# GpSimd's passes over normed rows and over q and k in pieces of 256 columns, and the q/k norm's factor inside the power

## The chip, the core and the metric

The kernel runs on one core of a Trainium2 chip. The time is the device time of one execution in microseconds; the median of several runs is compared. An execution of its own is taken with the hardware profiler and gives the trace.

## What is computed

One layer of a bidirectional encoder trunk for two groups of requests, a prompt of 4096 rows and a sample of 2048 rows, each of 1024 columns. Cut to what matters:

```python
def layer_norm(x, g, b):
    mu = x.mean(-1, keepdims=True)
    var = jnp.square(x - mu).mean(-1, keepdims=True)
    return (x - mu) * lax.rsqrt(var + 1e-5) * g + b

def l2norm(t):                       # each head's 64 values of q and of k
    return t * lax.rsqrt(jnp.sum(t * t, -1, keepdims=True) + 1e-6)

def mixer_layer(x, mem, w_in, ...):
    h = x @ w_in                     # one projection, split among three groups of heads
    y_attn = window_attention(aq, ak, av, sink, rel_bias) * silu(az)   # 8 heads, band of 3 blocks of 128
    y_dn = deltanet_branch(dn_q, dn_k, dn_v, a, b, ...) * silu(dn_z)   # short_conv, silu, l2norm(q), l2norm(k)
    y_mem = memory_attention(mq, mem @ w_mem_kv) * silu(mz)
    return concatenate([y_attn, y_dn, y_mem]) @ w_out

x = layer_norm(x, ln_in_g, ln_in_b); mem = layer_norm(mem, ln_in_g, ln_in_b)
x = layer_norm(2 ** 0.25 * x + mixer_layer(x, mem, ...), ln_g, ln_b)
```

## The kernel before

The 6144 rows are 48 tiles of 128 rows, handled in 24 pairs; another four tiles are the memory rows.

**The first part** (to about 1440 us) goes over the pairs. For each tile, `front` (from line 819) loads 1024 columns of f32 into `x` (three buffers), takes the statistics on VectorE (`bst`, `bmv`), the power of the variance on GpSimd (`brs`), the scale and shift on ScalarE, and then the gain and the bias in two passes on GpSimd over all 1024 columns (lines 825 and 826, the tiles `x<-x,grow` and `x<-x,brow`). ScalarE rounds the rows to f16 and VectorE takes the rest (`xhl`); a DMA transposes both (`xT`). `proj` (line 1235) multiplies with the weights on TensorE (`psf`, `psq`, `psk`). `attention` (line 1305) makes logits (`pslg`), adds the bias and takes the maximum on VectorE (`lg`, `mx`), the exponential on ScalarE, splits into two f16 halves (`aphl`), transposes by DMA (`apt`) and multiplies with v (`psov`). `conv` (line 1414), for the pair before, runs the five-tap convolution on VectorE (`acc`), silu, the split (`cfh`), a DMA transpose (`raw`), and for each tile the norm of q and k (lines 1434 to 1455): GpSimd adds the two halves (`n<-raw`, two passes of 256), ScalarE squares, VectorE sums 64 at a time and adds eps (`nss`), GpSimd takes the power -1/2 of 8 values per row, VectorE multiplies them by 1024, GpSimd multiplies 512 columns by them (`n<-n,nss`), and the result is split (`kqtm`) and stored. GpSimd also adds up v (`v<-raw`).

**The second part** runs both directions of the delta rule with their triangular inverses on GpSimd (`nb`, `tb`), the gates, the memory attention, the output projection (`pso`) and the last norm. None of its instructions is in the diff.

**The order.** No engine instruction is issued as it is written down. `Plan` (from line 56) collects the operations of a part with their dependences, gives each a cost from formulas (on GpSimd 200 ns plus 2.1 ns for each column, or 1.66 with a broadcast operand; a power 348 ns plus 165 for each column), and sorts them by a list scheduler, one queue for each engine and one for SyncE's DMAs; ranks come from a run backwards, seven schedules are made, and the one with the shortest planned end is issued. Its formulas have no term for engines that hold each other off. A list is ordered and issued when a pool closes: once for the first part (line 1620), once for the second. Each engine works its queue strictly in order. All instructions carry line 505, where the sorted list is issued; in the views they are told apart by their tiles.

Of the kernel before, what the change touches and what calls it, by code (L numbers as in the profile page):

```python
# [14 lines left out]
ALU = mybir.AluOpType  # L15
# [4 lines left out]
P = 128  # L20
D = 1024
# [529 lines left out]
def encoder(ctx: ExitStack, tc: tile.TileContext, A, outs):  # L551
    nc = tc.nc
    plan = Plan(tc)
    V, S, G, T, Q = plan.engines()
# [21 lines left out]
    def sc1(name):  # L576
        nscal[0] += 1
        return scal[:, nscal[0] - 1:nscal[0]]
# [212 lines left out]
    def layer_norm_stats(pool, x, eps, tag):  # L791
        st = pool.tile([P, 2, 6], F32, tag=tag + "st", name="bst")
        for i in range(2):
            V.bn_stats(st[:, i, :], x[:, i * 512:(i + 1) * 512])
        mv, rs = norm_scale(pool, st, eps, tag)
        nb = pool.tile([P, 1], F32, tag=tag + "nb", name="bnb")
        V.scalar_tensor_tensor(nb, mv[:, 0:1], -1.0, rs, op0=ALU.mult, op1=ALU.mult)
        return rs, nb
# [9 lines left out]
    def split(eng_hi, dst_h, dst_l, src, scale=None):  # L808

        if scale is None:  # L810
            S.activation(dst_h, src, AF.Copy)
            V.tensor_tensor(dst_l, src, dst_h, op=ALU.subtract)
        else:
            S.activation(dst_h, src, AF.Copy, scale=scale)
            V.scalar_tensor_tensor(dst_l, src, scale, dst_h, op0=ALU.mult, op1=ALU.subtract)

    grow_in, brow_in = grow, brow

    def front(pool, src_rows, xT_out, hl_dram=None, x_dram=None):

        x = gx.tile([P, D], F32, tag="x", name="x", bufs=3)
        Q.dma_start(out=x, in_=src_rows)
        rs, nb = layer_norm_stats(pool, x, LN_EPS, "f")
        S.activation(x, x, AF.Identity, scale=rs, bias=nb)
        G.tensor_tensor(x, x, grow_in, op=ALU.mult)
        G.tensor_tensor(x, x, brow_in, op=ALU.add)
        hl = pool.tile([P, 2, D], F16, tag="xhl", name="xhl", bufs=1)
        split(None, hl[:, 0, :], hl[:, 1, :], x)
        flat = hl.rearrange("p a b -> p (a b)")
        if xT_out is not None:  # L830
            Q.dma_start_transpose(out=xT_out, in_=flat)
        if hl_dram is not None:
            Q.dma_start(out=hl_dram, in_=flat)
        if x_dram is not None:
            Q.dma_start(out=x_dram, in_=x)
# [264 lines left out]
    def front_tile(t):  # L1100
        src = seqs[seq_of[t]][0][pos_of[t] * P:(pos_of[t] + 1) * P, :]
        front(pa, src, xT_of[t // 2][:, t % 2], x_dram=x32_d[t])
        if t % 2:
            Q.dma_start(out=xT_d[t // 2], in_=xT_of[t // 2])
# [91 lines left out]
    eps_k = sc1("eps_k")  # L1196
# [217 lines left out]
    def conv(pp):  # L1414

        c = cb[pp]
        raws = []
        for f0 in (0, 2, 4):
            acc = pa.tile([P, 2, 256], F32, tag="acc", name="acc", bufs=2)
            for f in range(2):  # L1420
                S.activation(acc[:, f], c[:, f0 + f, 0:256], AF.Copy, scale=cw[:, f0 + f, 0:1])
                for j in range(1, 5):
                    V.scalar_tensor_tensor(acc[:, f], c[:, f0 + f, j:j + 256], cw[:, f0 + f, j:j + 1], acc[:, f],
                                           op0=ALU.mult, op1=ALU.add)
            th = pa.tile([P, 2, 256], F32, tag="cth", name="cth", bufs=1)
            S.activation(th, acc, AF.Tanh, scale=hisk)
            V.scalar_tensor_tensor(acc, th, 1.0, acc, op0=ALU.add, op1=ALU.mult)
            fh = pa.tile([P, 2, 2, 256], F16, tag="cfh", name="cfh", bufs=1)
            split(None, fh[:, 0], fh[:, 1], acc)
            raw = pa.tile([P, 2, 2, 2, P], F16, tag="raw" if f0 < 4 else "rawv", name="raw", bufs=4 if f0 < 4 else 2)  # L1430
            Q.dma_start_transpose(out=raw.rearrange("p a f t c -> p (a f t) c"),
                                  in_=fh.rearrange("p a f t -> p (a f t)"))
            raws.append(raw)
        for tb in range(2):
            t = 2 * pp + tb
            n32 = pa.tile([P, 2, 4, 64], F32, tag="n32", name="n32", bufs=1)
            sq = pa.tile([P, 2, 4, 64], F32, tag="nsq", name="nsq", bufs=1)
            ss = pa.tile([P, 2, 8], F32, tag="nss", name="nss", bufs=2)
            for i in range(2):
                G.tensor_tensor(n32[:, i].rearrange("p (f h) d -> p f (h d)", f=2), raws[i][:, 0, :, tb, :],  # L1440
                                raws[i][:, 1, :, tb, :], op=ALU.add)
            S.activation(sq, n32, AF.Square)
            V.tensor_reduce(ss[:, 0], sq.rearrange("p q h d -> p (q h) d"), axis=AX.X, op=ALU.add)
            V.tensor_scalar(ss[:, 0], ss[:, 0], eps_k, None, op0=ALU.add)
            G.tensor_tensor(ss[:, 1], ss[:, 0], nhalf.to_broadcast([P, 8]), op=ALU.pow)
            V.tensor_scalar(ss[:, 1], ss[:, 1], 1024.0, None, op0=ALU.mult)
            n3 = n32.rearrange("p q h d -> p (q h) d")
            G.tensor_tensor(n3, n3, ss[:, 1].unsqueeze(2).to_broadcast([P, 8, 64]), op=ALU.mult)
            kqtm = pa.tile([P, 4, 2, 2, 64], F16, tag="kqtm", name="kqtm", bufs=1)
            o = kqtm.rearrange("p h t s d -> p t h s d")  # L1450
            split(None, o[:, :, :, 0, :], o[:, :, :, 1, :], n32)
            v32 = pa.tile([P, 4, 64], F32, tag="v32", name="v32", bufs=1)
            G.tensor_tensor(v32.rearrange("p (f h) d -> p f (h d)", f=2), raws[2][:, 0, :, tb, :],
                            raws[2][:, 1, :, tb, :], op=ALU.add)
            Q.dma_start(out=dst_d[t], in_=kqtm)
            Q.dma_start(out=dn_d[t], in_=n32)
            Q.dma_start(out=dv_d[t], in_=v32)
# [21 lines left out]
    def dn_back(pool, psp, dr, tiles, ds, emit_out):  # L1479
        for i, (t, d) in enumerate(zip(tiles, ds)):  # L1480
            dn_level(pool, psp, dr, i % NPAR, d)
            first = pos_of[t] == 0 if dr == 0 else pos_of[t] == lens[seq_of[t]] - 1
            if first:
                dn_reset(pool)
            po = dn_chain(pool, psp, dr, d)
            emit_out(t, po)

    units = [lambda m=m: front(pa, seqs[m // 2][1][(m % 2) * P:(m % 2 + 1) * P, :], None, xm_d[m])
             for m in range(4)]

# [14 lines left out]
    for i in range(NP + 1):  # L1505
        plan.rank = RK[6]
        if i + 1 < NP:
            front_pair(i + 1)
        if i < NP:
            plan.rank = RK[0]  # L1510
            proj(i)
        plan.rank = RK[2]
        if i > 0:
            conv(i - 1)
            plan.rank = RK[3]
            attention(2 * i - 1)
        if i < NP:
            plan.rank = RK[4]
            attention(2 * i)
        plan.rank = RK[5]  # L1520
        if i == min(NP, max(NG // 2, NP - FIRST)):
            gates(0, pa, (("oat", 2), ("qktm", 2), ("nsq", 1)))
            fr += dn_front([Alias(None, early)], Alias(None, {"fr": (pj, "pw", 1)}), 0, [todo[0][1]], step=1)
        for _ in range(min(len(units), -(-len(units) // max(1, NP - 3 - i)))):
            units.pop(0)()
# [308 lines left out]
```

## Time and profile before

| | |
|---|---|
| median of three runs | 3352.14 us (3349.26 to 3354.52) |
| the profiled execution | 3363.07 us, of which the span 3361.0 us |
| TensorE matmul busy | 2870.1 us, 85% |
| VectorE busy | 2920.9 us, 87% |
| ScalarE busy | 2441.2 us, 73% |
| GpSimd busy | 1711.0 us, 51% |
| chain of waits | VectorE 31%, TensorE 20%, GpSimd 15%, DMA 13%, issue 10%, ScalarE 8% |

Busy is the time in which an engine has an instruction under way; it holds time in which that instruction itself is held up. The chain of waits goes back from the last instruction, at each step to what released it or to the instruction before it on its engine. PE is TensorE, DVE VectorE, ACT ScalarE, POOL GpSimd, SPq SyncE's queue of DMAs. `out<-in` names the tiles that an instruction writes and reads.

### The profile page before, as it was taken

What the parts mean: (1) busy time and instruction counts of PE and PEld (TensorE: products, weight loads), DVE (VectorE), ACT (ScalarE), POOL (GpSimd) and SP (SyncE); (2) the same over time, 40 slices, a digit from 0 to 9 for tenths busy, and PEclk for the clock granted to TensorE, in tenths of its full rate; (3) what the DMA queues carried; (4) which work ended last, traced back from release to release, by engine and by line L of the source; (5) the groups of instructions that cost most, each with busy time, mean ns of one, the idle gap of its engine ahead of it and who ended that gap; (6) DMA issues with size and microseconds to landing.
All of it is one profiled execution on the core that took longest, in us unless ns stands there. A gap on an engine that the chain in (4) does not pass through costs nothing.

```text
span 3361.0 us, 82755 instructions
## 1 busy us (share of the span) xinstructions
PE 2870.1 (85%) x29856; PEld 1893.3 (56%) x29856; DVE 2920.9 (87%) x6850; ACT 2441.2 (73%) x6253; POOL 1711.0 (51%) x2611
## 2 busy tenths in 40 slices
PE   5788888788898887767899999999988988998988
PEld 4566666666676665444556555555554544444544
DVE  7999868799999989678889888888878988888997
ACT  4577656767777776688888878777877777777764
POOL 3644424344444334546645455455528666657662
PEclk9899998899999998878999999999998999999999
DMA  6999999999999999898678887778788777877775
GB/s 203 239 224 220 219 222 222 234 230 220 212 233 220 200 224 247 210 223 180 165 191 194 206 181 178 172 161 181 172 190 194 191 183 179 193 179 188 183 175 154
DMA packets 1336916, 671.43 MB, mean 200 GB/s; under 512 B 1127728, under 2 KB 1243312, under 8 KB 1332280
## 3 DMA queue, kind: packets, MB, share of 16 engines
q1 hardware_dynamic: 1336504, 666.14, 86.3%
q8 instruction: 234, 3.83, 0.5%
q14 instruction: 178, 1.46, 0.1%
HBM read 240.12 MB, written 181.49 MB: 125 GB/s over the span
## 4 chain that ended last, share of the span: by engine, by line
DVE 31%; PE 20%; POOL 15%; DMA 13%; issue 10%; ACT 8%; SPq 3%; POOLq 0%; ACTq 0%; DVEq 0%
POOL nb L505 5%; DVE acc L505 5%; POOL tb L505 5%; PE pso L505 5%; PE psg L505 5%; PE psf L505 3%; SPq L505 3%; DVE lg L505 3%; DVE aphl L505 3%; PE psk L505 2%; ACT lg L505 1%; PE psq L505 1%; DMA uc<-ud 1%; PE pslg L505 1%; DVE rx L505 1%
## 5 line engine op out<-in xcount | busy, mean ns | idle before, releaser
L505 PEld LDWEIGHTS <-xT 128*128 128x128 f16 x5760 | 535.5, 99 | 385.2 <-issue 52.5
L505 PE MATMUL psg<-w2a,xT 128*128 128x512 f16 (+1 forms) x2304 | 446.0, 334 | 9.6 <-DVE qtm L505 8.0
L505 PE MATMUL psf<-xT,w1f 128*128 128x256 f16 (+1 forms) x3600 | 439.9, 276 | 14.7 <-DMA xT<-xhl 6.3
L505 PEld LDWEIGHTS <-w1f 128*128 128x128 f16 x3600 | 341.7, 101 | 59.4 <-issue 10.8
L505 POOL TENSOR_TENSOR nb<-nb,tb 128x30 f32<-128x30 f32 (+6 forms) x750 | 348.6, 465 | 49.3
L505 POOL TENSOR_TENSOR tb<-nb,na 128x30 f32<-128x30 f32 (+6 forms) x750 | 342.6, 457 | 48.3
L505 ACT ACTIVATE lg<-lg,mx,scal 128x385 f32<-128x385 f32 (+1 forms) x384 | 263.8, 688 | 122.3 <-DVE mx L505 107.6
L505 PE MATMUL pslg<-kfm,qfm 128*128 128x128 f16 x2240 | 201.0, 233 | 164.1 <-DVE mx L505 149.4
L505 DVE SCALAR_TENSOR_TENSOR acc<-cb,cw,acc 128x256 f32<-128x256 f32 x576 | 329.8, 605 | 4.1 <-POOL cb L505 1.7
L505 PEld LDWEIGHTS <-qfm 128*128 128x128 f16 x2624 | 204.2, 104 | 222.3 <-issue 188.0
L505 PEld LDWEIGHTS <-yT 128*128 128x128 f16 x2304 | 200.1, 99 | 216.1 <-issue 27.7
L505 PE MATMUL pso<-w2a,yT 128*128 128x512 f16 x1152 | 311.4, 394 | 9.6 <-DMA yT<-yhl 7.1
L505 PE MATMUL pso<-w2b,yT 128*128 128x512 f16 x1152 | 298.9, 383 | 0.0
L505 PE MATMUL psg<-w2b,xT 128*128 128x512 f16 x1152 | 289.3, 382 | 3.8 <-DMA w2b<-w_d 3.8
L505 PE MATMUL psq<-w1t,xT 128*128 128x512 f16 x1152 | 287.0, 385 | 0.2 <-ACT cb L505 0.2
L505 DVE TENSOR_TENSOR aphl<-lg,aphl 128x768 f16<-128x768 f32 (+1 forms) x192 | 209.9, 1096 | 49.7 <-ACT aphl L505 49.3
L505 POOL TENSOR_TENSOR n<-raw 128x256 f32<-128x256 f16 x96 | 82.3, 867 | 262.2 <-DMA raw<-cfh 62.1
L505 DVE CUSTOM_DVE_ANT_0 lg<-pslg,bias 128x385 f32<-128x385 f32 (+1 forms) x384 | 195.3, 539 | 17.7 <-PE pslg L505 13.5
L505 POOL TENSOR_TENSOR x<-x,grow 128x1024 f32<-128x1024 f32 x52 | 128.0, 2462 | 121.8 <-ACT x L505 117.6
L505 PEld LDWEIGHTS <-th 64*64 64x64 f16 x2304 | 99.1, 111 | 131.1 <-issue 106.1
L505 PE MATMUL psk<-w1t,xT 128*128 128x272 f16 x1152 | 161.4, 287 | 13.5 <-DVE qktm L505 10.0
L505 PE MATMUL psx<-rx,th 64*64 64x64 f16 x2304 | 126.8, 197 | 41.3 <-DVE rx L505 29.8
(1026 smaller groups left out, 7607.8 us busy)
## 6 DMA issues: line engine op xcount, KB each, us to landing
x<-x SPq DMA_DIRECT2D x48, 512.0 KB, 4.3
xT<-xT SPq DMA_DIRECT2D x24, 1024.0 KB, 5.5
xT<-xT SPq DMA_DIRECT2D x48, 512.0 KB, 4.5
n<-dn SPq DMA_DIRECT2D x96, 256.0 KB, 3.3
r<-x SPq DMA_DIRECT2D x48, 512.0 KB, 4.4
out_dram<-r SPq DMA_DIRECT2D x48, 512.0 KB, 3.8
cr<-crow SPq DMA_DIRECT2D x47, 512.0 KB, 5.1
yhl<-yhl SPq DMA_DIRECT2D x48, 384.0 KB, 3.4
```

The source lines that it names most:

```text
L505: getattr(self.eng[o["e"]], o["name"])(*o["args"], **o["kw"])
```

## The change

In `front` the two passes of 1024 columns become eight of 256, gain and bias in turn for each quarter; 52 tiles go through it. In `conv` the sum with eps is multiplied by 2^-20 in the same instruction, so that the power -1/2 gives 2^10 times what it gave; the instruction that multiplied by 1024 is gone; the pass over q and k is made in two of 256 columns, q first, then k. It is done for 48 tiles.

```diff
@@ front
         S.activation(x, x, AF.Identity, scale=rs, bias=nb)
-        G.tensor_tensor(x, x, grow_in, op=ALU.mult)
-        G.tensor_tensor(x, x, brow_in, op=ALU.add)
+        for c in range(0, D, 256):
+            xc = x[:, c:c + 256]
+            G.tensor_tensor(xc, xc, grow_in[:, c:c + 256], op=ALU.mult)
+            G.tensor_tensor(xc, xc, brow_in[:, c:c + 256], op=ALU.add)
@@ conv
-            V.tensor_scalar(ss[:, 0], ss[:, 0], eps_k, None, op0=ALU.add)
+            V.tensor_scalar(ss[:, 0], ss[:, 0], eps_k, 2.0 ** -20, op0=ALU.add, op1=ALU.mult)
             G.tensor_tensor(ss[:, 1], ss[:, 0], nhalf.to_broadcast([P, 8]), op=ALU.pow)
-            V.tensor_scalar(ss[:, 1], ss[:, 1], 1024.0, None, op0=ALU.mult)
-            n3 = n32.rearrange("p q h d -> p (q h) d")
-            G.tensor_tensor(n3, n3, ss[:, 1].unsqueeze(2).to_broadcast([P, 8, 64]), op=ALU.mult)
+            for i in range(2):
+                G.tensor_tensor(n32[:, i], n32[:, i], ss[:, 1, 4 * i:4 * i + 4].unsqueeze(2).to_broadcast([P, 4, 64]),
+                                op=ALU.mult)
```

## Rows read from the trace of the kernel before

**Rows 1.** Stages: length, PE, PEld, DVE, ACT, POOL busy, clock, DMA share, GB/s.
```profile
120.00:1320.00 1200.00, 1001.21 (x10942) 784.29 (x10941) 1076.70 (x2435) 850.26 (x2041) 510.68 (x389) 0.94 1.02 221
...
1440.00:3361.00 1921.00, 1708.61 (x17562) 1002.76 (x17562) 1667.13 (x3963) 1470.15 (x3950) 1089.34 (x2068) 0.95 0.79 183
```

**Rows 2.** Chain of waits, 120 to 1320 us, shares of that stretch.
```profile
by line: issue 14.7%; DVE acc L505 13.7%; DVE lg L505 8.0%; DVE aphl L505 7.3%; PE psf L505 6.6%; ACT lg L505 3.9%; PE psq L505 3.6%; PE pslg L505 3.0%; DVE mx L505 2.8%; DVE nss L505 2.7%; SPq L505 2.7%; DVE bst L505 2.3%; DVE cfh L505 2.1
```

**Rows 3.** Waits of PE, 120 to 1320 us: total, times, longest.
```profile
PE pslg L505 <- DVE mx L505: 136.0, 82, 8.1
PE psm L505 <- DMA wm<-wm_d: 13.2, 10, 2.9
```

**Rows 4.** Timeline, DVE and POOL near 263 us: start, length, engine, instruction.
```profile
263.08 2.36 POOL L505 TENSOR_TENSOR x<-x,brow 128x1024 f32<-128x1024 f32 x1
263.51 2.74 DVE L505 TENSOR_TENSOR aphl<-lg,aphl 128x768 f16<-128x768 f32 x1 [3.25 <-ACT aphl L505]
265.39 1.40 POOL L505 TENSOR_TENSOR n<-raw 128x256 f32<-128x256 f16 x1
```

**Rows 5.** Timeline: first and last of 96 VectorE instructions beside x passes.
```profile
12.62 3.10 DVE L505 TENSOR_TENSOR sq<-stg 128x768 bf16<-128x768 f32 x1
...
1278.53 2.40 DVE L505 SCALAR_TENSOR_TENSOR acc<-cb,cw,acc 128x256 f32<-128x256 f32 x1
```

**Rows 6.** Tile x, its passes: shortest/median/longest ns, first and last start.
```profile
L505 POOL TENSOR_TENSOR x<-x,grow x52: 2342/2366/3393, 12.2 to 1273.1; 128x1024 f32<-128x1024 f32 x52
L505 POOL TENSOR_TENSOR x<-x,brow x52: 2328/2404/3211, 15.0 to 1278.3; 128x1024 f32<-128x1024 f32 x52
```

**Rows 7.** Pieces of the chain of waits with held VectorE time, first and last.
```profile
43.07 3.25 DVE sq L505 x3
...
1273.28 2.24 DVE mx L505
```

**Rows 8.** Tile yd, its passes of 256 columns (second part).
```profile
L505 POOL TENSOR_TENSOR yd<-of,yd x48: 719/729/1742, 2521.3 to 3338.3; 128x256 f32<-128x256 f32 x48
```

**Rows 9.** Timeline: first, last VectorE instruction beside n<-raw, then beside v<-raw.
```profile
193.68 0.77 DVE L505 SCALAR_TENSOR_TENSOR acc<-cb,cw,acc 128x256 f32<-128x256 f32 x1
...
1369.46 0.90 DVE L505 SCALAR_TENSOR_TENSOR acc<-cb,cw,acc 128x256 f32<-128x256 f32 x1
...
233.65 1.42 DVE L505 TENSOR_TENSOR aphl<-lg,aphl 128x768 f16<-128x768 f32 x1
...
1419.68 0.67 POOL L505 TENSOR_TENSOR v<-raw 128x256 f32<-128x256 f16 x1
1419.76 1.14 DVE L505 TENSOR_TENSOR kqtm<-n,kqtm 128x512 f16<-128x512 f32 x1
```

**Rows 10.** Tile n, GpSimd's passes: shortest/median/longest ns.
```profile
L505 POOL TENSOR_TENSOR n<-raw x96: 661/794/2247, 128.4 to 1422.9; 128x256 f32<-128x256 f16 x96
...
L505 POOL TENSOR_TENSOR kg<-n,egs x96: 607/615/1792, 1451.3 to 2384.9; 128x256 f32<-128x256 f32 x96
...
L505 POOL TENSOR_TENSOR n<-n,nss x48: 1038/1144/1914, 146.1 to 1427.8; 128x512 f32<-128x512 f32 x48
```

**Rows 11.** Groups of POOL, 120 to 1320 us: busy us, mean ns, idle before.
```profile
L505 POOL TENSOR_TENSOR n<-raw 128x256 f32<-128x256 f16 x86 | 74.9, 881 | 229.3 <-DMA raw<-cfh 55.2 <-DVE kqtm L505 54.6 <-DMA dn<-n 39.9
```

**Rows 12.** Chain of waits, pieces of x on POOL: first and last of six.
```profile
63.12 2.33 POOL x L505
...
1190.02 2.31 POOL x L505
```

**Rows 13.** Tile nss, the multiplication by 1024.
```profile
L505 DVE TENSOR_SCALAR nss<-nss x48: 153/172/2332, 145.8 to 1427.5; 128x8 f32<-128x8 f32 x48
```

**Rows 14.** Group of DVE, 0 to 1440 us: busy, mean ns, idle before.
```profile
L505 DVE SCALAR_TENSOR_TENSOR acc<-cb,cw,acc 128x256 f32<-128x256 f32 x576 | 329.8, 605 | 4.1 <-POOL cb L505 1.7 <-ACT acc L505 1.3
```

**Rows 15.** DMA issues of the page: KB each, median us to landing.
```profile
x<-x SPq DMA_DIRECT2D x48, 512.0 KB, 4.3
...
r<-x SPq DMA_DIRECT2D x48, 512.0 KB, 4.4
```

## The prediction

> **What bounds the kernel now.** I read the busy times by stage first. The two lists that the planner orders show as two parts: the change touches only the first, which ends near 1440 us, and the 1921 us behind it are ordered from a list that the diff does not alter [rows 1]. So every term lies in 0 to 1440 us, and nearly all of it in the steady stage from 120 to 1320 us. There VectorE is busy for 1076.7 of 1200 us, TensorE for 1001.2 and GpSimd for 510.7 [rows 1]. The chain of waits of that stage is led by VectorE: acc, lg, aphl, mx, nss, bst and cfh alone give 38.9% of it [rows 2]. TensorE's largest idle cause there is VectorE emptying a logits bank (136.0 us); the largest one that is a transfer is 13.2 us [rows 3]. VectorE bounds the stage; GpSimd is idle for more than half of it.
>
> Next I read what VectorE's time is made of, in the order of time. At 263.51 us the subtraction of aphl starts beside an x pass of GpSimd and lasts 2.74 us, ending 0.81 us after the pass; the next GpSimd instruction, begun at 265.39, is drawn out to 1.40 us and ends only after aphl does [rows 4]. So the two engines hold each other off for whole instructions and take turns. Of VectorE's instructions in 0 to 1440 us that last over 100 ns longer than the median of their form, 96 overlap an x pass; 93 of the 104 passes hold one, and the excess over the medians sums to 151.6 us, or 1.46 us for each pass. The first and the last stand in [rows 5]. The median pass is 2.37 or 2.40 us [rows 6]. Traced along the chain, 80.8 us of the 151.6 lie on it, in 68 pieces, the first of them inside the sq piece and the last large one at mx [rows 7]. That is 53%.
>
> **The change, part by part.** *The x passes.* 104 passes of 1024 columns become 416 of 256. The trace has a pass of just that shape, f32 with two full operands: yd, median 729 ns [rows 8]. Four take 2.92 us where one took 2.38, so GpSimd works 416 x 0.729 - 104 x 2.38 = 56 us longer, beside an idle half.
>
> The disputed number is how long a piece holds VectorE. The trace has no x piece, so I bound it by passes of nearly this length in the same stage. The 96 passes that add raw into n (median 794 ns, shortest 661) hold VectorE for 15.6 us by the same count, 42 instructions, 162 ns a pass; the 48 that fill v from raw hold it for 13.9 us, 34 instructions, 290 ns a pass; first and last of each stand in [rows 9], the durations in [rows 10]. Scaled by 729/670 (670 being their undisturbed length, as v shows at 1419.68) these are 176 and 316 ns, and I take the middle, 246 ns: some pieces will follow each other closely as v follows n, others will stand alone. Then 416 x 0.246 = 102 us against 151.6: VectorE gains 49 us. With the 53% that lies on the chain that is **-26 us**; by the two ends 73 and 131 us are held, giving -42 and -11 us.
>
> Against it stands GpSimd's own waiting. In the stage the raw passes take 881 ns in the mean [rows 11] where the undisturbed ones take 670, so 0.2 us each is waiting for VectorE. A piece then takes 0.93 us, the eight of a tile 7.4 us against 5.0. Who waits: the copy to xhl, the transpose behind it, and whatever stands behind the pieces on GpSimd (nss, brs, n). On the chain the x passes have six pieces, 14.0 us, first and last in [rows 12]; lengthened by 49% they cost **+7 us**. The transfers and TensorE come later by at most these 2.4 us a tile, which the idle half of GpSimd and the three x buffers cover; without that cover it would be 52 x 2.4 = 125 us.
>
> The Trainium skill, "Perfetto Trace Analysis", section "Optimizing Scalar/DVE Operations", speaks against pieces: it says that grouping work into larger operations can raise throughput where the engine is saturated, because each instruction has a fixed cost. The fixed cost shows here too, by the 729 ns above; but the engine whose passes are cut is not the saturated one. If GpSimd bounded the stage the rule would decide, and the 56 us would be the sum.
>
> *The q/k norm.* The pass over q and k, 48 of 512 columns at a median of 1.14 us, becomes 96 of 256 with a broadcast operand, which kg does in 615 ns [rows 10]: +0.09 us each, 4 us of GpSimd in all, off the chain. It holds VectorE for 19.7 us now; 96 x 0.246 x 615/729 = 20 us later. Zero.
>
> *The factor.* The addition of eps takes the factor 2^-20 as its second operation, and the power gives 2^10, exact powers of two; the separate multiplication by 1024 goes. It is 48 instructions of 172 ns in the median [rows 13], 8.3 us of VectorE, also on the way from power to pass, so there is one turn from engine to engine less. Half on the chain: **-4 us**. Its longest is 2332 ns, because it too is held at times; that part is already in the sum above and moves to the instruction behind it, so it is not counted twice.
>
> *The order.* 52 x 6 + 48 - 48 instructions more, and other planned costs, mean that all of the first list is sorted anew: GpSimd, SyncE and VectorE queues may all stand in another order between 0 and 1440 us. The planner knows nothing of the holding. No row prices this; VectorE's 123 us of idle time in the stage [rows 1] is what the present order leaves, and I allow a sixth of it, 20 us, either way and zero in the sum.
>
> Sum: -26 + 7 - 4 = -23 us. On the profiled execution (span 3361.0, 3363.07 us with what lies around it) that is 3340 us; the median of the three runs is 10.9 us lower, 3352.14, and gives **3329 us**.
>
> **Rivals.** *The turn-taking eats it (slower).* When VectorE has one two-input instruction after another, as in the acc runs, every piece finds one waiting, and eight pieces hold longer than two passes do. The point from which this decides is plain: 151.6/416 = 364 ns a piece, half its length. At 450 ns the held time is 187 us, +35 us, on the chain +19; with +7 and -4 the time is 3374 us; with every piece held in full, 303 us, the same sum gives +83 us, 3435 us. For: 93 of 104 passes hold something, and after the first turn the engines are in step. Against: v, which follows other passes closely, has 316 ns scaled, and lg, bst and qktm are not drawn out, so they break the runs. The Trainium skill ("SBUF — State Buffer", section "SBUF: two separate sides") words the rule behind this rival: a VectorE instruction with two SBUF inputs and a GpSimd instruction that reads SBUF exclude one another, and whichever starts first keeps the shared ports for its whole length. The trace agrees: aphl ends behind the pass.
>
> *The gain is hidden.* The DMA engines show a mean share of 1.02 in the stage and 0.79 behind it [rows 1]. If they set the pace, or if the next stage's work on TensorE is late by as much, VectorE's 49 us only turn into idle time: 3350 us. Against: a 512 KB transfer lands in 4.3 us in the first part and in 4.4 us in the last [rows 15], so nothing queues, and TensorE hardly waits for transfers [rows 3].
>
> *More than the chain's share.* Held time off the chain delays others too. At 176 ns a piece, with all of 78 us returned and 8 us for the factor, the time is 3266 us.
>
> *The pieces don't stay together.* If the planner sorts urgent work (the power of nss, brs) between pieces, nss and brs come earlier by up to one pass; that is a gain within the forecast's range.
>
> **How the numbers follow.** The forecast case, 3293 (176 ns, order 20 us for it) to 3364 us (316 ns, order against it), has 0.57: most of it lies below 3345, so 0.51 faster and 0.06 no change. The larger gain has 0.07, the hidden gain 0.14, turn-taking 0.22 (0.21 slower, 0.01 no change). Within 0.2%, 6.7 us, is about what a measurement of this kernel can tell from no change. Faster 0.58, same 0.21, slower 0.21. The range reaches from 3280, a part of the larger gain, to 3374, the turn-taking at 450 ns; what is left out is its worse half and the best of the larger gain.
>
> **What would show it.** Right: VectorE instructions held by x pieces sum to about 100 us, none longer than 0.75 us plus its own work; acc's mean in the first part falls from 605 ns [rows 14] by some 40; the second list starts some 20 us sooner; x pieces average near 0.9 us. Wrong: held time near or over 150 us (turn-taking); held time down but the first part as long, with TensorE or ScalarE waiting for GpSimd's n, brs or x (its queue is late), or for transfers (hidden); or the first part changed by idle time of VectorE, not by its work (the order).

## The result, and the profile after

The changed kernel takes 3298.93 us in the median (3296.42 to 3300.31) beside 3350.7 us for the kernel before: a ratio of 0.9845, with a 95% interval of 0.9828 to 0.9862, or 52 us less. The forecast was 3329 us, 23 us less. Its sign was right and the time lies in its range, but the gain is 2.3 times as large as the one that was worked out. All differences in us from a run's ratio below are taken on about 3350 us; the changed kernel, measured a second time (e15), came to 58 us less by its ratio, so two such figures can differ by 6 us without a cause.

**Where the time went.** The two parts of the kernel can be timed by a landmark: the first `n64h` of the second list on ScalarE. These rows are the groups of tile n, before and then after; the columns are shortest/median/longest ns, first and last start in us.

```profile
L505 ACT ACTIVATE n64h<-n x192: 292/306/310, 1438.3 to 3299.0; 32x128 f16<-32x128 f32 x192
```
```profile
L505 ACT ACTIVATE n64h<-n x192: 292/306/310, 1383.7 to 3234.9; 32x128 f16<-32x128 f32 x192
```

The landmark comes 54.6 us sooner. The profiled execution of before was 12 us above its own median, and 9 of those us lie behind the landmark (3361.0 - 1438.3 = 1922.7 us there, 1913.9 after). On every engine the order of the second list is the same in both kernels. So the 52 us came out of the first part, as the prediction had placed it.

The same stretch by engines, up to the landmark, before and then after: length, busy us (instructions) of PE, PEld, DVE, ACT, POOL, then granted clock, DMA share, GB/s.

```profile
0.00:1438.30 1438.30, 1161.24 (x12292) 890.38 (x12292) 1252.04 (x2882) 969.36 (x2298) 621.70 (x543) 0.93 0.98 222
```
```profile
0.00:1383.70 1383.70, 1154.51 (x12292) 884.46 (x12292) 1185.96 (x2833) 971.21 (x2299) 734.28 (x903) 0.94 1.02 231
```

This is the pair of rows to read first. VectorE is busy for 66.1 us less, idle for 11.5 us more (186.3, then 197.7), and 66.1 - 11.5 is the 54.6. Some 12 of the 66.1 belong to the norm (e6 below), the others to the pieces. TensorE is busy for 7 us less and ScalarE for 2 us more, with the same work. GpSimd is busy for 113 us more, but the waits of ScalarE and VectorE for it add up to 85 us before and 89 after.

Most of what VectorE no longer loses is holding. In tile x of after, GpSimd's pieces stand where the passes of [rows 6] stood:

```profile
L505 POOL TENSOR_TENSOR x<-x,grow x208: 713/733/1717, 13.0 to 1222.2; 128x256 f32<-128x256 f32 x104
L505 POOL TENSOR_TENSOR x<-x,brow x208: 714/902/1718, 15.4 to 1223.6; 128x256 f32<-128x256 f32 x104
```

VectorE's convolution step, tile acc of after, and one of its small instructions, tile mx of before and of after:

```profile
L505 DVE SCALAR_TENSOR_TENSOR acc<-cb,cw,acc x576: 425/476/1043, 64.5 to 1333.4; 128x256 f32<-128x256 f32 x192
```
```profile
L505 DVE TENSOR_SCALAR mx<-mx,scal x96: 196/220/2318, 120.2 to 1422.6; 128x4 f32<-128x4 f32 x96
```
```profile
L505 DVE TENSOR_SCALAR mx<-mx,scal x96: 206/222/751, 110.8 to 1368.7; 128x4 f32<-128x4 f32 x96
```

The gain pieces take 733 ns in the median, nearly the 729 ns of yd [rows 8]; the bias pieces, of the same shape, take 902 ns: they too are held. acc's longest is 1043 ns, its own 476 and most of one piece; mx's longest was 2318 ns and is 751, its own 222 and less than one piece. By the count of the prediction 210 VectorE instructions are held on 193 of the 416 pieces, for 86.4 us in all, where it was 151.6. The first and the last, in the timeline of after:

```profile
13.41 1.48 DVE L505 TENSOR_TENSOR sq<-stg 128x768 bf16<-128x768 f32 x1
...
1221.61 0.69 DVE L505 TENSOR_SCALAR mx<-mx,scal 128x4 f32<-128x4 f32 x1
```

The relief is not spread evenly. By the same count aphl is held for 9.1 us instead of 26.6, mx for 9.3 instead of 19.7, cfh for 5.4 instead of 12.1. The convolution step acc hardly gains: 98 of its instructions are held for 42.7 us, half of all that is left, where 25 were held for 48.7 us. Within a run of them the two engines do take turns, as the group of acc after and one such run show (timeline of after; seven steps in 5.21 us, 744 ns each instead of 476):

```profile
L505 DVE SCALAR_TENSOR_TENSOR acc<-cb,cw,acc 128x256 f32<-128x256 f32 x576 | 319.0, 584 | 5.6 <-POOL cb L505 2.1 <-ACT acc L505 1.9
```
```profile
793.55 5.21 DVE L505 SCALAR_TENSOR_TENSOR acc<-cb,cw,acc 128x256 f32<-128x256 f32 x7
794.58 1.78 POOL L505 TENSOR_TENSOR x<-x,grow 128x256 f32<-128x256 f32 x2
796.32 1.77 POOL L505 TENSOR_TENSOR x<-x,brow 128x256 f32<-128x256 f32 x2
```

The chain of waits of the profile after breaks off 170 us before the end of the span, so it is not read here; from here on the account is VectorE's busy and idle time up to the landmark.

### The profile page after: what moved, and what is told of

Read it like the earlier page. It is cut to its first block, busy times and chain, and to the rows that moved or that the text cites. A ratio compares the mean times of both kernels' runs of the same rounds, so it can differ in the third digit from the quotient of the medians.

```text
span 3297.6 us, 83056 instructions
## 1 busy us (share of the span) xinstructions
PE 2852.4 (86%) x29856; PEld 1882.0 (57%) x29856; DVE 2852.1 (86%) x6802; ACT 2442.7 (74%) x6253; POOL 1826.1 (55%) x2971
## 5 line engine op out<-in xcount | busy, mean ns | idle before, releaser
L505 POOL TENSOR_TENSOR nb<-nb,tb 128x30 f32<-128x30 f32 (+6 forms) x750 | 356.2, 475 | 49.3
L505 DVE SCALAR_TENSOR_TENSOR acc<-cb,cw,acc 128x256 f32<-128x256 f32 x576 | 319.0, 584 | 5.6 <-POOL cb L505 2.1
L505 POOL TENSOR_TENSOR x<-x,grow 128x256 f32<-128x256 f32 x208 | 176.7, 865 | 117.4 <-ACT x L505 105.0
L505 DVE TENSOR_TENSOR aphl<-lg,aphl 128x768 f16<-128x768 f32 (+1 forms) x192 | 195.4, 1018 | 53.1 <-ACT aphl L505 52.6
L505 POOL TENSOR_TENSOR x<-x,brow 128x256 f32<-128x256 f32 x208 | 189.4, 927 | 0.0
```

Of the source, the lines that this page charges most:

```text
L505: getattr(self.eng[o["e"]], o["name"])(*o["args"], **o["kw"])
```

## Experiments

Two theories stood first. **A:** the shorter holding is the gain, in whatever order. **B:** the planner's new order is the gain. They are told apart by a square: each order with whole passes and with pieces. Where a kernel keeps an order, the planner is given the same list, and only what is issued at a place differs.

### Pieces at the old order (e1)

```diff
         G.tensor_tensor(x, x, grow_in, op=ALU.mult)      # planned as before
+        plan.ops[-1]["emit"] = pieces(grow_in, ALU.mult)  # issued as four passes of 256
...                                                        # the bias likewise
```

> The planner's list and its order are those of the kernel before; each x pass is issued at its place as four passes of 256 columns (four gains where the gain stood, four biases where the bias stood); the norm is as before. Theory A (holding): the gain comes from VectorE being held for shorter pieces, in any order. The held time beside x passes falls from 152 to 80 to 110 us and the kernel takes 3300 to 3320 us. Theory B (order): the new order of the first list made the gain. The time stays within 10 us of 3351, held time or not.

Measured: 0.9898 (0.988 to 0.9915), 34 us less. Held 91.8 us. The stretch to its landmark:

```profile
0.00:1400.80 1400.80, 1150.92 (x12292) 882.68 (x12292) 1199.58 (x2882) 971.46 (x2298) 709.83 (x855) 0.94 1.00 228
```

VectorE is busy for 52.5 us less than before, idle for 15 us more, and the part is 37.5 us shorter. Shorter holding at an unchanged order, with what GpSimd's longer work takes back, gives two thirds of the gain.

### The new order with whole passes (e2)

```diff
         for c in range(0, D, 256):
             G.tensor_tensor(xc, xc, grow_in[:, c:c + 256], op=ALU.mult)
+            plan.ops[-1]["emit"] = (lambda: None) if c else whole(grow_in, ALU.mult)
...
```

> The counterpart: the order of the changed kernel, but at the first piece of a tile's gain and of its bias one pass of 1024 columns is issued, and nothing at the other six. The norm is as in the changed kernel. Theory A (holding): VectorE is held for about 150 us beside x passes again and the time goes back to 3335 to 3350 us. Theory B (order): the time stays within 10 us of 3299.

Measured: 1.001 (0.9996 to 1.0023). Held 154.2 us. The order of the changed kernel, with its norm, gains nothing while the passes are whole. B falls; but pieces are worth 34 us at the old order and 55 at the new one with the new norm, so order and norm are not idle either.

### The change in its two halves (e3, e4)

e3 is the hunk of `front` alone, e4 the hunk of `conv` alone, each planned anew.

> Only the x passes in pieces, planned anew; norm and factor as before. Theory A: nearly all of the 52 us, 3300 to 3312 us. The prediction's own terms would give 3352 - 26 + 7 = 3333 us. Rival C (norm): the norm's shorter chain has the missing half of the gain; then this gives about 3330 us.

> Only the norm: factor inside the power and two passes of 256 over q and k, planned anew; x passes of 1024 as before. Theory A: 3340 to 3350 us (some 8 us of VectorE less). Rival C (norm): 3320 to 3330 us. A new order alone may move it by some us either way.

Measured: e3 0.9887 (0.987 to 0.9903), 38 us less; e4 1.0044 (1.0028 to 1.0061), 15 us more. e3 ends at the upper edge of A's 3300 to 3312 us; e4, at 3367.39 us, is outside what A and C gave it. The halves sum to 23 us less, together they give 52. A halved change that is planned anew is a third schedule, not half of the change; this pair shows how large that effect is, and can't price the norm.

### The norm at a fixed order (e6, e7)

e6 puts the old norm at its places in the new order, e7 the new norm at its places in the old one.

```diff
# e7
             V.tensor_scalar(ss[:, 1], ss[:, 1], 1024.0, None, op0=ALU.mult)
+            plan.ops[-1]["emit"] = lambda: None     # planned, not issued
...
```

> The order of the changed kernel with its x pieces; the norm as before: eps alone, the power, the multiplication by 1024 on VectorE just ahead of the pass over q and k, and that pass whole at the place of its first half. Theory E (norm): 3312 to 3320 us. Theories D and F: 48 VectorE instructions of 0.17 us come back, 3299 to 3308 us.

> The order of the kernel before with whole x passes; only the norm is changed, at its old places: factor with eps, no multiplication by 1024, the pass over q and k in two halves one behind the other. The prediction's term: 8.3 us of VectorE, half of it on the chain, -4 us: 3340 to 3346 us. Theory E (norm): -12 us or more. The planned-anew norm alone took 15 us more than the kernel before; if that was its order, as I hold, this one is not slower than before.

Measured: e7 0.9993 (0.998 to 1.0006), no difference that can be told, and an interval that holds the foretold 4 us; e6 0.9878 (0.9865 to 0.9891), which is 11 us above the changed kernel (4 to 18 by the two intervals); its 3307.19 us lie where D (urgent work between the pieces) and F (the new order as a whole) put it, not E (the norm as the cause of all that e1 lacks). The new norm is worth nothing that shows with whole passes and about 11 us beside the pieces; e4's 15 us were its order. In e6 VectorE is busy for 1197.85 us to the landmark at 1392.8, 11.9 us over the changed kernel, and idle for 194.9:

```profile
0.00:1392.80 1392.80, 1157.02 (x12292) 885.23 (x12292) 1197.85 (x2882) 972.30 (x2299) 721.31 (x855) 0.94 1.02 229
```

### How much there is to take (e8)

```diff
         G.tensor_tensor(x, x, grow_in, op=ALU.mult)
+        plan.ops[-1]["emit"] = lambda: None     # gain and bias planned, not issued
...
```

> Leaves out part of the computation: gain and bias of the input norm are not applied; everything else stands at its place in the order of the kernel before. No x pass holds VectorE (152 us less), GpSimd works 259 us less, a tile's rows are ready 5 us sooner. At the prediction's 53% of held time: 3350 - 81 = 3270 us. If held time comes back nearly in full: 3200 to 3225 us. This is the most that any splitting of these passes could give at this order.

Measured: 3269.33 us, 0.9764 (0.975 to 0.9778): 81 us less by the medians, 53% of the 151.6, the very number expected. But the way to it is not a fixed share:

```profile
0.00:1349.10 1349.10, 1147.05 (x12292) 873.27 (x12292) 1096.09 (x2882) 973.36 (x2299) 346.27 (x439) 0.95 1.05 237
```

VectorE is busy for 156 us less and idle for 67 us more. Of the VectorE time freed, e1 gets back 37.5 of 52.5 us (71%), the changed kernel 54.6 of 66.1 (83%), this one 89.2 of 156 (57%), and e9 below 25.6 of 29.9 (86%). None of these is the share of held time alone: GpSimd is busy for 88 us more in e1, 113 in the changed kernel, 32 in e9 and 275 us less here, and in the changed kernel the norm and the order are in it too. At the old order the share falls with the time that is freed (e9, e1, this run), pieces of 128 apart. What VectorE waits for when more is freed can be read here: for ScalarE 158.5 us (107.6 before), for transfers 36.8 (12.5), for TensorE 25.0 (22.2).

### Other sizes at the old order (e9, e10)

As e1, in pieces of 512 and of 128 columns.

> As e1, but each x pass in two pieces of 512 columns, at the old order. If VectorE meets a pass after some 0.95 us of work of its own (the one figure that fits both 1.46 us held for a pass of 2.37 us and 0.22 us for a piece of 0.73 us), a piece of 1.27 us holds 0.57 us: 118 us in all against 152 and 92. At 53% of it: 3350 - 17 = 3333 us. If the gain came only from pieces short enough to slip between VectorE's own instructions: 3345 to 3352 us.

> As e1, but in eight pieces of 128 columns, some 0.46 us each. By the same figure a piece holds 0.095 us, 79 us in all: 3350 - 38 = 3312 us, no better than e1 by more than 7 us. GpSimd works some 1.3 us longer for each pass than in one piece; if its lengthening costs anything like the prediction's term, 3320 to 3330 us. If turn-taking decides at this size: held time over 92 us again and slower than e1.

Measured: e9 0.9939 (0.9917 to 0.9962), 20 us less, held 119.2 us where 118 were expected (first row below); e10 1.0029 (1.0015 to 1.0042), 10 us more, though held time is down to 53.3 us; its 3358.58 us are far from the 3312 and the 3320 to 3330 that were expected. The stretches of e9 and of e10, and ScalarE's wait for x in it (total, times, longest us):

```profile
0.00:1412.70 1412.70, 1158.79 (x12292) 886.06 (x12292) 1222.16 (x2882) 971.30 (x2299) 653.73 (x647) 0.94 1.00 226
```
```profile
0.00:1448.20 1448.20, 1164.16 (x12292) 891.32 (x12292) 1168.66 (x2882) 969.29 (x2298) 793.28 (x1271) 0.93 0.97 221
```
```profile
ACT xhl L508 <- POOL x L832: 93.2, 28, 14.9
```

The same wait in the kernel before:

```profile
ACT xhl L505 <- POOL x L505: 13.5, 2, 13.0
```

In e10 VectorE's busy time is 83 us lower than before and its idle time 93 us higher. GpSimd works 172 us longer, in a queue whose order was made for 622 us of work, and ScalarE waits for its x, for its n (kqtm, 39.9 us, 21.6 before) and for its raw sums (nsq, 33.0, 13.8 before). Turn-taking did not decide (a piece holds 64 ns on average). That GpSimd's length did is argued from these waits; e12 below, where the planner knows the length, agrees.

### GpSimd's length alone (e11)

```diff
         G.tensor_tensor(x, x, brow_in, op=ALU.add)
+        # issued behind it: a power of 8 columns and one of 1 column into a tile that nothing reads
...
```

> The kernel before at its order, with two more GpSimd instructions behind each tile's bias pass: a power of 8 columns and one of 1 column into a tile that nothing reads, some 2.3 us a tile, as much as the pieces were said to lengthen GpSimd's work. Powers do not hold VectorE (none of the 48 nss powers is among the passes that held it). This prices the prediction's term of GpSimd's longer work alone: by it +7 us, 3358 us; if the idle half covers it, 3345 to 3353 us; if work behind it on GpSimd's queue is late, 3365 us or more.

Measured: 1.0068 (1.0046 to 1.0089), 23 us more. Held time is unchanged (151.7 us), and so is VectorE's busy time:

```profile
0.00:1458.70 1458.70, 1169.03 (x12292) 895.89 (x12292) 1251.00 (x2882) 970.13 (x2299) 750.85 (x647) 0.93 0.96 219
```

129 us of GpSimd's time cost 21 us of idle VectorE, three times the prediction's term for 125 us, although GpSimd is idle for half of the stretch. Its idle half is not cover: the queue is strictly in order, and what is late on it is late for ScalarE and VectorE, whose waits for GpSimd grow from 85 to 128 us. The powers stand behind a tile's passes, so x itself is hardly later: ScalarE waits 18.3 us for it. In e1 that wait is 51.3 us and in e10 93.2. So this run prices the queue behind the passes, not a later x.

### Planned for 128 columns (e12)

The changed kernel with 128 in place of 256.

> The changed kernel with x pieces of 128 columns, planned anew. If finer places for urgent GpSimd work are worth more still: 3280 to 3295 us. If held time is what counts and the order only moves it: 3295 to 3310 us. Above 3310 us: GpSimd's longer work or turn-taking costs more than the pieces give.

Measured: 0.9836 (0.9813 to 0.9859), the same as the changed kernel within the intervals; its 3293.43 us lie at the border between the two expected bands, so they do not choose. The size that loses 10 us at the old order is as good as any when the planner orders for it: held 62.3 us, GpSimd busy for 838 us.

### Why the new order pays with pieces (e5, e13, e14)

e5 is the changed kernel's order, with each tile's four gains issued together where the first stood, and its four biases likewise, so that nothing is issued between the four; this tests D, E and F of the norm's runs above. e13 is e1, with the planner told 2950 ns for a pass. e14 is the changed kernel, with the planner told 588 ns for a piece, so that four count as one whole pass did. e15 repeats the changed kernel beside them.

> The order of the changed kernel on every engine, but a tile's four gain pieces are issued together where the first of them stood, and its four bias pieces where the first bias piece stood; so the 81 other GpSimd instructions that the planner put between pieces now wait for whole groups, as they would for whole passes. Theory D (interleaving): the 20 us that the changed kernel has beyond the pieces at the old order come from urgent work sorted between pieces; then 3312 to 3322 us. Theory E (norm): they come from the norm; then 3297 to 3304 us. Theory F (the new order as a whole, no one place): also 3297 to 3306 us.

> Norm as before. The planner keeps two x passes for a tile, but is told 2950 ns for each (what it counts for four pieces) instead of 2350; each is issued as four pieces of 256 at its place. Theory G (the planner knows the length): the new order starts x earlier and places GpSimd's other work for a longer pass, so ScalarE and VectorE wait for GpSimd some 85 to 110 us in the first part (157 in e1) and the kernel takes 3300 to 3310 us. Theory H (places between pieces): waits stay near 150 us and the time near e1, 3313 to 3322 us.

> The changed kernel, but the planner is told 588 ns for each x piece, so that four count as much as one whole pass did. Its list, its places between pieces and its norm are those of the changed kernel; only the planned length is the old one. Theory G: ScalarE and VectorE wait for GpSimd some 130 us or more, 3310 to 3325 us. Theory H: 3297 to 3305 us, waits near 90 us.

> The changed kernel once more beside these two on one chip, for their differences: 3294 to 3304 us.

Measured: e15 0.9827 (0.9807 to 0.9846); e5 0.989 (0.9874 to 0.9905), 15 us above the first measurement of the changed kernel; e13 0.9898 (0.9877 to 0.992), as e1; e14 0.9919 (0.9901 to 0.9937), 31 us above e15. The stretches of e5, e13 and e14:

```profile
0.00:1393.60 1393.60, 1161.05 (x12292) 885.98 (x12292) 1180.29 (x2833) 970.45 (x2299) 723.89 (x903) 0.94 1.01 229
```
```profile
0.00:1397.30 1397.30, 1153.15 (x12292) 881.99 (x12292) 1199.79 (x2882) 969.05 (x2299) 716.50 (x855) 0.94 1.02 228
```
```profile
0.00:1416.70 1416.70, 1160.88 (x12292) 886.58 (x12292) 1198.00 (x2834) 970.38 (x2299) 726.42 (x903) 0.94 1.00 225
```

e5 falls between what D and what E and F gave it. Of G (the planner knows the length) and H (places between the pieces), neither holds alone. With places between the pieces but the old length planned (e14), VectorE is idle for 218.7 us and the waits of ScalarE and VectorE for GpSimd are 111 us. With the length known but no places (e13), these waits are cut from 157 us in e1 to 81, and yet VectorE's idle time is 197.5 us against 201. With both it is 197.7, and its busy time is 14 us lower than in e13, 12 of which e6 gives to the new norm. Grouping the pieces at the new order (e5) costs 16 us of idle time and saves 6 us of busy time. By the landmarks, the 54.6 us are 37.5 for pieces at the old order (e1), 8.0 for the new order (from e1 to e6, both with the old norm) and 9.1 for the norm (from e6 to the changed kernel); the landmark of e15 is 2.6 us from that of the first execution, so the two small ones are uncertain by some us. Other orders cost more than this one gives: with pieces of 256, 15 us (e5) and 31 (e14); and with 128, e12 lies 65 us below e10, the norm's part in it. So an order has to suit its pieces, and the changed kernel's does; why exactly this one does is left open.

## Why the prediction fell short

- **What bounds the kernel: right.** The first part gave it all, and by VectorE's time; TensorE and ScalarE hardly changed.
- **How long a piece holds: slightly too long.** 246 ns were taken, 208 measured (86.4 us over 416; 221 in e1). The bounds of 176 and 316 ns from [rows 9] hold it. This makes 65 us freed instead of 49.
- **The share that comes back: the step that failed.** The prediction turned held time into time by the 53% of it that lay on the chain [rows 7]. With the measured 65 us its own sum would have been -35 + 7 - 4 = -32 us; 52 came. Of the VectorE time that was freed, 71% came back at the old order (e1) and 83% in the changed kernel, after what GpSimd's longer work takes. It was not that the pieces relieved just the instructions on the chain: if each instruction's relief counts by the part of its held time that lay on the chain before, 30 of the 65 us would come back, or 46%. The chain names one way through the waits; that held time beside it moved the next step as well is the reading that is left, and it is argued, not shown. The rival "more than the chain's share" described this and had a chance of 0.07. The 53% that e8 gives is no proof of the share, since that run also spares GpSimd 275 us.
- **GpSimd's longer work, +7 us: too small.** At the old order as much extra time on GpSimd costs 23 us (e11). The pieces take 0.90 us in the mean, near the 0.93 us reckoned, and GpSimd is busy with x for 107 us more; in the changed kernel, where no run prices it by itself, VectorE's idle time rose by 11.5 us in all. The prediction set the fixed cost of each instruction aside because GpSimd is not the saturated engine; yet at an unchanged order pieces of 128 lose 10 us (e10), and with an order made for them they don't (e12).
- **The norm, -4 us: probably too small beside pieces,** about -11 us (e6, 4 to 18), and not to be told from zero with whole passes (e7).
- **The order, zero and 20 us either way: it lay within the 20 here.** The new order gave some 8 us with pieces (from e1 to e6). But 20 us does not bound what an order can do: e14 lost 31 us by it.
- **The rivals.** Turn-taking, the rival that would have decided at 364 ns a piece, came in part: in the runs of acc, as it had said, but 208 ns a piece in the mean. The gain was not hidden by transfers: their share rose to 1.02 in the first part with the time still falling, and it was 1.05 in e8.
- **Signs named beforehand.** Held time is 86 us for the foretold 100, none longer than 0.75 us plus its own work, and x pieces average 0.90 us. acc's mean fell from 605 ns [rows 14] to 584, by half of the 40 foretold, because acc itself is still held for 42.7 us; the second list starts 54.6 us sooner, not 20.
- **That the time lies in the range is its width.** 3299 us is near the lower end of the forecast case, 3293, which stood for a piece of 176 ns and an order 20 us better. Neither was so; a larger share and a larger norm took their place.

With the measured sizes the sum at the old order is 52.5 us of VectorE less 15 us of idle time, -37 us, and with the new order and norm, 17 us by the landmarks, -55, for which the medians show -52.

## What to carry to other kernels

When two engines exclude each other for the length of an instruction, cut the long passes of the one that has time, and judge it by the full one's busy time (long against median durations of one form); here the share of the stall on one chain was too low. Expect little where the full engine has one instruction after another that must wait, as in the runs of acc. Then count the cut engine's extra length as a cost of its own, since an in-order queue with idle time is still late, and let the order be made with the new lengths. Don't price a part of a change by planning that part anew: keep the order and change only what is issued.

## What the runs showed of the hardware

The held time of VectorE for each GpSimd pass of f32 with two operands in SBUF, at one order (before, e9, e1, e10), falls faster than its length: 1.46 us for 1024 columns (2.37 us long), 0.573 for 512 (1.28 us), 0.221 for 256 (0.73 us), 0.064 for 128 (0.46 us). If the work that VectorE does before it comes to an instruction that must wait is spread exponentially with a mean of 0.95 us, these would be 1.50, 0.58, 0.22 and 0.10 us: a fit to three of the four, not a mechanism shown. The lengths, tile x of e9 and then of e10:

```profile
L832 POOL TENSOR_TENSOR x<-x,grow x104: 1257/1280/2254, 12.1 to 1249.3; 128x512 f32<-128x512 f32 x104
```
```profile
L832 POOL TENSOR_TENSOR x<-x,grow x416: 447/459/1489, 12.7 to 1284.9; 128x128 f32<-128x128 f32 x139
```

GpSimd's powers of 8 columns and of 1 hold VectorE for no time that shows: 104 more of them left its busy time at 1251.0 us against 1252.0 (e11). And instructions with a single tensor operand are held like those with two: mx with its scalars for 2318 ns above, and nss times a constant for 2332 [rows 13], both beside an x pass. The Trainium skill ("SBUF — State Buffer", section "Who interferes with whom") says that tensor_scalar can run in a mode that uses the shared ports and then contends; the trace agrees that these contend; in which mode they ran no run here shows.
